# A two-layer diffusion backbone on one core: the last three steps of an attention head moved into the turn between two heads

## The chip, the cores and the metric

One core of a Trainium2 chip (trn2) runs the whole program. Its engines run side by side, and in the trace each runs its instructions in the order in which the program issued them: PE (TensorE, matrix products; PEld is its loading of weights), DVE (VectorE), ACT (ScalarE), POOL (GpSimd) and SP (which issues DMA transfers). The metric is device microseconds (us) of one execution, the median of several.

## The reference

Two layers over 512 latent tokens and 256 context tokens, width 1024, all in 32-bit floats. What matters here is the attention with two softmaxes and a difference, for 8 heads:

```python
z_lat = h_lat @ w_in[l];  kv_ctx = z_ctx[..., B_K:C_IN]       # in the last layer only k and v of the context
q, k = rope(rmsnorm(q)), rope(rmsnorm(k))                      # k of the context: rmsnorm alone
s = einsum('bqahd,bkahd->bahqk', q, k) * B_QK_DIM ** -0.5      # a: two score maps a head
p = softmax(s);  a = p[:, 0] - lam * p[:, 1]
attn = einsum('bhqk,bkhe->bqhe', a, v)                         # 768 keys for latent queries
```

In layer 0 the 256 context queries attend to the 256 context keys as well; in layer 1 there are no context queries. Around it stand a gated branch, a short convolution branch, an output projection and a feed-forward part.

## The kernel before, in words

Every product is done in three passes of split operands: a number is a rounded part ("hi") and the rest ("lo"), and hi*hi, lo*hi and hi*lo are added up. So a product of 128 rows by 8 blocks is 24 matmuls, and each operand needs a copy on ACT (the hi part) and a subtraction on DVE (the lo part). Weights stream in by DMA; the class `Stream` casts their hi part on ACT (`whi`, line 83) and subtracts for the lo part on DVE (`wlo`, line 69; the call `tick` after each step of a weave puts a pending one into DVE's queue).

The order of the work is written out by hand. Generators issue a piece of work and yield a number, its cost; `weave` (line 37) always advances the generator whose yielded sum is the smallest share of its given total. The order in which instructions are issued is the order in which each engine runs them.

In the attention of a layer, heads follow each other. While head h does its attention (`attn`, line 891), the projections of head h+1 are issued (`project`, line 1323), woven with it. `project` is: `qk_proj` (q and k for 6 blocks of 128 tokens in layer 0; in layer 1, 4 blocks and one product for the context keys, which come out the wrong way round and are transposed by `kc_tr`, lines 673 to 678), then `v_proj` in eight pieces (four of 6 matmuls with 512 columns, four of 6 with 256; called pieces 1 to 8 below), and between those pieces, on DVE, `qk_norm` (12 or 13 tiny instructions), and three `qk_rope` (called rope 0, 1, 2). Then comes a turn (line 1340): `qk_tr` transposes the three parts of q and k on PE, ACT copies the hi part, DVE subtracts (line 729), and SP issues DMAs that build a swapped copy of q (`qw`, line 733). The turn is woven with one half of the short convolution branch (`fill`), which is plain PE work.

`attn` goes through tiles of 128 queries (4 of them in layer 1, 6 in layer 0, called tile 0, 1, ...). Step i does, in this order: `av` of the pair of tiles that ends with tile i-4 (odd tiles only; 18 matmuls in turns hi, lo, hi: lines 886, 887, 888; 6 matmuls for the context pair); `to_at` of tile i-3 (6 transposes on PE, line 874; ACT copies the hi part `ah`, line 878; DVE subtracts the lo part `al`, line 879); `scores` of tile i (8 matmuls, line 841; minimum on DVE, line 848; exponentials on ACT, line 850); `combine` of tile i-1 (DVE, lines 859 to 862). So with n tiles the steps run to n+3, and the last three have only `av` and `to_at` left. `ah` and `al` have one buffer. PE's results of all these pieces, score maps aside, share four banks of PSUM (pool `pmm`, line 1307), and a bank is free again when ACT and DVE have read it.

Of the kernel before, what the change touches and what calls it, by code (L numbers as in the profile page):

```python
# [3 lines left out]

# [1 line left out]

# [5 lines left out]
F32 = mybir.dt.float32  # L12
# [8 lines left out]
NL, NC, T, D = 512, 256, 768, 1024  # L21
# [12 lines left out]
N_VS = 2  # L34


def weave(*gens, tick=lambda: None):
    act = [[g, 0.0, float(tot)] for g, tot in gens]
    while act:
        act.sort(key=lambda e: e[1] / e[2])  # L40
        e = act[0]
        try:
            e[1] += next(e[0])
        except StopIteration:
            act.remove(e)
        tick()
# [83 lines left out]
class Net:  # L130
# [34 lines left out]
    def tick(self, n):  # L165
        for _ in islice(self.bg, n):
            pass
# [713 lines left out]
    def av(self, st, kt0, nkt, yb, t0):  # L881
# [6 lines left out]
            nc.tensor.matmul(po[:, :256], lhsT=vl, rhs=st["ah"][:, i, :], start=False, stop=(i == nkt - 1))  # L888
        nc.scalar.copy(yb[:, t0:t0 + 256], po[:, :256])

    def attn(self, l, h, pool, st):
        yb = self.slots.tile([128, T], F32, tag=f"A{h}", name="yb")
        self.yb[h] = yb
        seq = [(0, 0, T), (128, 0, T), (256, 0, T), (384, 0, T)]
        if l == 0:
            seq += [(512, 512, NC), (640, 512, NC)]

        n = len(seq)
        sc, am = {}, {}
        cost = self.attn_costs(l)  # L900
        for i in range(n + 4):
            left = cost[i]
            if i >= 4 and (i - 4) % 2:
                tt, kk, nn = seq[i - 4]
                self.av(st, kk // 128, nn // 128, yb, tt - 128)
                yield 1000
                left -= 1000
            if 0 <= i - 3 < n:
                self.to_at(st, am.pop(i - 3), seq[i - 3][2], (i - 3) % 2, pool)
                yield 700  # L910
                left -= 700
            if i < n:
                sc[i] = self.scores(pool, st, *seq[i])
            if 0 <= i - 1 < n:
                am[i - 1] = self.combine(*sc.pop(i - 1))
            if i == 0:
                for c in self.v_tr(l, h, pool, st):
                    yield c
                    left -= c
            yield left  # L920

    @staticmethod
    def attn_costs(l):
        return [3200] + [2200] * 3 + [1800] * 4 if l else [3200] + [2000] * 9

    def subln(self, l, pool):
        nc = self.nc
# [308 lines left out]
    def run(self):  # L1236
# [13 lines left out]
        with tc.tile_pool(name="const", bufs=1) as const, tc.tile_pool(name="w", bufs=1) as wp, \  # L1250
# [17 lines left out]
            for l in range(2):  # L1268
                t = const.tile([128, PC_N], F32, name=f"pc{l}")
# [24 lines left out]
            for l in range(2):  # L1294
                segs = S_LAT if l else S_FULL
                ap = None
# [10 lines left out]
                with tc.tile_pool(name="attn", bufs=1) as ap, tc.tile_pool(name="pmm", bufs=4, space=PSUM) as self.mm, \  # L1307
                        tc.tile_pool(name="ps", bufs=2, space=PSUM) as self.sp:
                    self.ws.late = True
                    st = [dict(h=h) for h in range(8)]  # L1310
                    tick = self.ws.low

                    def fill(count):
                        while count:
                            g = next(cgen, None)
                            if g is None:
                                return
                            yield from g
                            count -= 1

                    chalf = 7800 if l == 0 else 5200

                    def project(h):
                        yield from self.qk_proj(l, h, ap, st[h])
                        vp = self.v_proj(l, h, ap, st[h])
                        yield next(vp)
                        if l:
                            st[h]["kc"]()
                            yield next(vp)
                        if h == 0:  # L1330
                            self.attn_lam(l, ap, tabs[0])
                        self.qk_norm(l, h, ap, st[h])
                        yield next(vp)
                        yield next(vp)
                        for c in range(3):
                            st[h]["rope", c] = self.qk_rope(l, c, ap, st[h])
                            yield next(vp)
                        yield from vp

                    def turn(h):  # L1340
                        weave((self.qk_tr(l, h, ap, st[h]), 6800), (fill(1), chalf), tick=tick)

                    p0 = project(0)
                    for i in range(8):
                        if gb:
                            next(gb)
                        next(p0)
                        tick()
                        if i == 5:
                            self.attn_setup(l, ap, *tabs)  # L1350
                    weave((p0, 15000), (fill(1), chalf), tick=tick)
                    turn(0)
                    for h in range(8):
                        a = self.attn(l, h, ap, st[h]), sum(self.attn_costs(l))
                        if h < 7:
                            weave(a, (project(h + 1), 23500), tick=tick)
                            turn(h + 1)
                        else:
                            weave(a, (fill(99), (1 + N_VS) * 10.4 * (512 if l else 768)), tick=tick)
                self.ws.low()  # L1360
                self.ws.late = False
                mmp = psum_all()
# [26 lines left out]
                n = sum(s[1] for s in self.segs)  # L1389
                for k in range(8):  # L1390
                    t = xp.tile([128, T], F32, tag=f"x{k}", name="x")
# [158 lines left out]
```

## Time and profile before

| | |
|---|---|
| median of 3 runs (range) | 2700.38 us (2697.53 to 2700.61) |
| the profiled execution, its span | 2700.74 us, 2699.0 us |
| PE busy | 2618.6 us (97%) |
| DVE busy | 1661.3 us (62%) |
| ACT busy | 1011.8 us (37%) |
| attention, layer 0: turns of heads 0 to 7 begin | 111 us to 508 us, some 57 us apart |
| attention, layer 1: turns of heads 0 to 7 begin | 1652 us to 1976 us, some 46 us apart |

How to read it: busy times are unions of the instructions of an engine. The end of a matmul in the profile is modelled, and matmuls overlap in the pipeline, so distances between starts are used where exact stretches matter: in an undisturbed stream a matmul with 512 columns starts 0.23 us after the one before, one with 256 columns 0.12 us. Idle time is put down to what ended it.

### The profile page before, as it was taken

What the parts mean: (1) busy time and instruction counts of PE and PEld (TensorE: products, weight loads), DVE (VectorE), ACT (ScalarE), POOL (GpSimd) and SP (SyncE); (2) the same over time, 40 slices, a digit from 0 to 9 for tenths busy, and PEclk for the clock granted to TensorE, in tenths of its full rate; (3) what the DMA queues carried; (4) which work ended last, traced back from release to release, by engine and by line L of the source; (5) the groups of instructions that cost most, each with busy time, mean ns of one, the idle gap of its engine ahead of it and who ended that gap; (6) DMA issues with size and microseconds to landing.
All of it is one profiled execution on the core that took longest, in us unless ns stands there. A gap on an engine that the chain in (4) does not pass through costs nothing.

```text
span 2699.0 us, 37119 instructions
## 1 busy us (share of the span) xinstructions
PE 2618.6 (97%) x14952; PEld 2267.2 (84%) x14952; DVE 1661.3 (62%) x2895; ACT 1011.8 (37%) x1711; POOL 220.6 (8%) x202
## 2 busy tenths in 40 slices
PE   7999999999999999999999999999999999999999
PEld 3988888888888888888888878898877888888887
DVE  5676777756555547544544567878777555654544
ACT  3454445452112224322322335455554232342332
POOL 0000000001111110100100100000001122020101
PEclk9999999999999999999999999999999999999999
DMA  5211122114333331222222232211225545223233
GB/s 222 81 44 51 50 59 70 50 54 141 118 112 115 110 141 55 77 80 77 77 81 78 77 103 75 64 58 54 69 67 169 175 164 177 74 94 102 94 102 110
DMA packets 80941, 254.36 MB, mean 94 GB/s; under 512 B 10480, under 2 KB 20992, under 8 KB 80384
## 3 DMA queue, kind: packets, MB, share of 16 engines
q1 hardware_dynamic: 65792, 196.64, 22.6%
q0 software_dynamic: 14544, 55.07, 6.3%
q8 instruction: 118, 1.93, 0.3%
q14 instruction: 55, 0.45, 0.1%
q10 hardware_dynamic: 432, 0.27, 0.0%
HBM read 234.63 MB, written 6.82 MB: 89 GB/s over the span
## 4 chain that ended last, share of the span: by engine, by line
PE 84%; DVE 8%; ACT 4%; DMA 2%; issue 1%; SPq 0%; POOL 0%; ACTq 0%; DVEq 0%; POOLq 0%
PE mm L183 22%; PE mm L186 22%; PE mm L184 22%; PE S L841 3%; PE mm L647 2%; PE mm L648 2%; PE mm L649 2%; DVE wlo L69 2%; DVE al L879 1%; ACT pa L850 1%; PE mmT L887 1%; ACT whi L83 1%; PE mmT L888 1%; PE mmT L886 1%; DMA wraw<-w 1%
## 5 line engine op out<-in xcount | busy, mean ns | idle before, releaser
L183 PE MATMUL mm<-hh,whi 128*128 128x512 f32 (+1 forms) x2392 | 859.7, 359 | 13.4 <-ACT hh L376 11.4
L184 PE MATMUL mm<-hl,whi 128*128 128x512 f32 (+1 forms) x2392 | 822.2, 354 | 4.4 <-DVE hl L379 4.1
L186 PE MATMUL mm<-hh,wlo 128*128 128x512 f32 (+1 forms) x2392 | 754.8, 354 | 1.6 <-DVE wlo L69 1.6
L183 PEld LDWEIGHTS mm<-hh,whi 128*128 128x128 f32 x2392 | 454.3, 190 | 106.4 <-ACT hh L376 16.3
L184 PEld LDWEIGHTS mm<-hl,whi 128*128 128x128 f32 x2392 | 454.5, 190 | 69.4 <-DVE hl L379 9.8
L69 DVE TENSOR_TENSOR wlo<-wraw,whi 128x1024 fp32r<-128x1024 f32 x320 | 399.0, 1247 | 153.1 <-ACT whi L83 151.3
L186 PEld LDWEIGHTS mm<-hh,wlo 128*128 128x128 f32 x2392 | 416.0, 191 | 42.4 <-DVE wlo L69 3.7
L83 ACT CAST whi<-wraw 128x1024 fp32r<-128x1024 f32 x320 | 334.7, 1047 | 296.3 <-PE mm L184 249.8
L1003 DVE SCALAR_TENSOR_TENSOR cv<-mm,pc,cv 128x511 f32<-128x511 f32 (+1 forms) x132 | 86.8, 657 | 181.8 <-ACT cv L1002 180.8
L850 ACT ACTIVATE pa<-S,mn 128x768 f32<-128x768 f32 (+1 forms) x160 | 129.2, 812 | 163.2 <-DVE mn L848 139.7
L183 PE MATMUL mm<-ah,whi 128*128 128x512 f32 (+1 forms) x528 | 188.0, 356 | 0.0
L647 PE MATMUL mm<-whi,hh 128*128 128x256 f32 x640 | 184.2, 288 | 1.3 <-DVE cp L778 0.8
L649 PE MATMUL mm<-whi,hl 128*128 128x256 f32 x640 | 181.0, 283 | 0.0
L648 PE MATMUL mm<-wlo,hh 128*128 128x256 f32 x640 | 181.0, 283 | 0.0
L184 PE MATMUL mm<-al,whi 128*128 128x512 f32 (+1 forms) x528 | 180.0, 354 | 0.0
L186 PE MATMUL mm<-ah,wlo 128*128 128x512 f32 (+1 forms) x528 | 161.7, 355 | 0.0
L1002 ACT ACTIVATE cv<-mm,pc 128x512 f32<-128x512 f32 (+1 forms) x132 | 88.6, 704 | 177.0 <-PE mm L186 177.0
L1164 DVE SCALAR_TENSOR_TENSOR x<-mm,mod,x 128x512 f32<-128x512 f32 (+1 forms) x91 | 58.2, 659 | 139.7 <-PE mm L186 139.7
L1207 POOL TENSOR_TENSOR cv<-cv 128x768 f32<-128x768 f32 (+1 forms) x44 | 91.8, 2087 | 606.6 <-DVE cv L1005 420.7
L647 PEld LDWEIGHTS mm<-whi,hh 128*128 128x128 f32 x640 | 122.2, 191 | 3.2 <-ACT cp L776 1.0
L648 PEld LDWEIGHTS mm<-wlo,hh 128*128 128x128 f32 x640 | 122.5, 191 | 0.1
L649 PEld LDWEIGHTS mm<-whi,hl 128*128 128x128 f32 x640 | 122.3, 191 | 0.0
(232 smaller groups left out, 4049.9 us busy)
## 6 DMA issues: line engine op xcount, KB each, us to landing
wraw<-w SPq DMA_DIRECT2D x320, 512.0 KB, 3.6
araw<-ada POOLq DMA_DIRECT2D x80, 512.0 KB, 4.0
qw<-qk SPq DMA_DIRECT2D x160, 64.0 KB, 2.0
araw<-ada SPq DMA_DIRECT2D x16, 512.0 KB, 7.8
x<-xT SPq DMA_DIRECT2D x8, 384.0 KB, 5.9
srow<-sscr POOLq DMA_DIRECT2D x3, 1024.0 KB, 7.4
x<-xT POOLq DMA_DIRECT2D x8, 384.0 KB, 6.3
xscr<-x SPq DMA_DIRECT2D x8, 256.0 KB, 4.0
```

The source lines that it names most:

```text
L69: self.lo_eng.tensor_tensor(lo, raw, hi.bitcast(F32), ALU.subtract)
L83: self.nc.scalar.copy(hi, raw)
L183: nc.tensor.matmul(ps[:, :m], lhsT=hh, rhs=xh[:, o:o + m], start=st, stop=False)
L184: nc.tensor.matmul(ps[:, :m], lhsT=hh, rhs=xl[:, o:o + m], start=False, stop=False)
L186: nc.tensor.matmul(ps[:, :m], lhsT=hl, rhs=xh[:, o:o + m], start=False, stop=sp)
L647: nc.tensor.matmul(ps[:, :256], lhsT=hh[:, sl], rhs=hi[:, c:c + 256], start=(k == 0), stop=False)
L648: nc.tensor.matmul(ps[:, :256], lhsT=hh[:, sl], rhs=lo[:, c:c + 256], start=False, stop=False)
L649: nc.tensor.matmul(ps[:, :256], lhsT=hl[:, sl], rhs=hi[:, c:c + 256], start=False, stop=(k == 7))
L850: nc.scalar.activation(pa[:, :nk], ss[a], AF.Exp, bias=mn[:, a:a + 1], scale=-1.0, accum_out=sm[a])
L1002: nc.scalar.activation(dst[:, o:o + m], s, AF.Identity, scale=w[1], bias=bias)
L1003: nc.vector.scalar_tensor_tensor(dst[:, o + 1:o + m], s[:, :m - 1], w[0], dst[:, o + 1:o + m], ALU.mult, ALU.add)
L1207: nc.gpsimd.tensor_tensor(cs[1][:, :n], cs[1][:, :n], cs[0][:, :n], ALU.mult)
```

## The change

`attn` now ends after step n (its last `combine`). The three steps that only hold `av` and `to_at` become a generator of their own, `attn_tail`, which the turn of the next head weaves with `qk_tr` and `fill`. For the last head of a layer, which has no next turn, `attn` and the tail follow each other as before, in one weave with what is left of `fill`. The costs that steer the weaves change: each step of `attn` counts 2000 (step 0: 3200), in both layers, so 15200 in layer 0 and 11200 in layer 1 against 23500 for the projections of the next head (before: 21200 and 17000); the tail counts 8000; `qk_tr` counts 5200 where it counted 6800. In layer 1 the transposes of the context keys are issued after piece 2 of `v_proj` where they were after piece 1, and `qk_norm` after piece 3 where it was after piece 2; the ropes stay where they were. No instruction is added or removed.

```diff
+    def attn_step(self, l, i, pool, st):
+        seq = self.attn_seq(l)
+        n = len(seq)
+        sc, am = st["sc"], st["am"]
+        if i >= 4 and i % 2:
+            tt, kk, nn = seq[i - 4]
+            self.av(st, kk // 128, nn // 128, st["yb"], tt - 128)
+            yield 1000
+        if 0 <= i - 3 < n:
+            self.to_at(st, am.pop(i - 3), seq[i - 3][2], (i - 3) % 2, pool)
+            yield 700
+        if i < n:
+            sc[i] = self.scores(pool, st, *seq[i])
+        if 0 <= i - 1 < n:
+            am[i - 1] = self.combine(*sc.pop(i - 1))
+
     def attn(self, l, h, pool, st):
...
+        for i in range(n + 1):
+            left = 2000
+            for c in self.attn_step(l, i, pool, st):
+                yield c
+                left -= c
             if i == 0:
                 for c in self.v_tr(l, h, pool, st):
-                    yield c
-                    left -= c
+                    yield 600
+                left += 0
             yield left
 
-    @staticmethod
-    def attn_costs(l):
-        return [3200] + [2200] * 3 + [1800] * 4 if l else [3200] + [2000] * 9
+    def attn_cost(self, l):
+        return 2000 * (len(self.attn_seq(l)) + 1) + 1200
+
+    def attn_tail(self, l, pool, st):
+        n = len(self.attn_seq(l))
+        for i, left in ((n + 1, 2600), (n + 2, 4000), (n + 3, 1400)):
+            for c in self.attn_step(l, i, pool, st):
+                yield c
+                left -= c
+            yield left
...
                         yield next(vp)
                         if l:
+                            yield next(vp)
                             st[h]["kc"]()
                             yield next(vp)
...
                         self.qk_norm(l, h, ap, st[h])
                         yield next(vp)
-                        yield next(vp)
+                        if not l:
+                            yield next(vp)
...
                     def turn(h):
-                        weave((self.qk_tr(l, h, ap, st[h]), 6800), (fill(1), chalf), tick=tick)
+                        g = [(self.attn_tail(l, ap, st[h - 1]), 8000)] if h else []
+                        weave(*g, (self.qk_tr(l, h, ap, st[h]), 5200), (fill(1), chalf), tick=tick)
...
-                        a = self.attn(l, h, ap, st[h]), sum(self.attn_costs(l))
+                        a, cost = self.attn(l, h, ap, st[h]), self.attn_cost(l)
                         if h < 7:
-                            weave(a, (project(h + 1), 23500), tick=tick)
+                            weave((a, cost), (project(h + 1), 23500), tick=tick)
                             turn(h + 1)
                         else:
-                            weave(a, (fill(99), (1 + N_VS) * 10.4 * (512 if l else 768)), tick=tick)
+                            a = chain(a, self.attn_tail(l, ap, st[h]))
+                            weave((a, cost + 8000), (fill(99), (1 + N_VS) * 10.4 * (512 if l else 768)), tick=tick)
```

## Rows read from the trace of the kernel before

**Rows 1.** The page, busy time of the engines (share of the span, instructions).

```profile
PE 2618.6 (97%) x14952; PEld 2267.2 (84%) x14952; DVE 1661.3 (62%) x2895; ACT 1011.8 (37%) x1711; POOL 220.6 (8%) x202
```

**Rows 2.** The waits of the seven whole head periods of layer 0 (120 to 518 us): who waited for whom, us in total, times, longest.

```profile
PE mmT L886 <- ACT ah L878: 11.2, 7, 1.6
PE mmT L887 <- DVE al L879: 11.2, 7, 1.6
```

**Rows 3.** The same of the seven head periods of layer 1 (1660 to 1982 us).

```profile
PE mmT L887 <- DVE al L879: 6.6, 7, 1.0
PE mmT L676 <- ACT kc L671: 4.2, 7, 0.6
PE S L841 <- DMA qw<-qk: 3.5, 6, 1.0
```

**Rows 4.** Timeline of PE in layer 0 near the end of head 1 (start us, duration us; in brackets idle time before it and what ended it).

```profile
208.05 0.40 PE L186 MATMUL mm<-hh,wlo 128*128 128x512 f32 x1
210.05 0.39 PE L886 MATMUL mmT<-ah,vh 128*128 128x256 f32 x1 [1.60 <-ACT ah L878]
212.03 0.58 PE L887 MATMUL mmT<-al,vh 128*128 128x256 f32 x1 [1.59 <-DVE al L879]
```

**Rows 5.** Timelines of DVE and of ACT in the same stretch.

```profile
209.56 0.69 DVE L638 TENSOR_REDUCE ss<-sq 128x8 f32<-128x512 f32 x1 [2.11 <-ACT sq L637]
210.16 1.22 DVE L69 TENSOR_TENSOR wlo<-wraw,whi 128x1024 fp32r<-128x1024 f32 x1
211.29 1.01 DVE L879 TENSOR_TENSOR al<-mmT,ah 128x512 fp32r<-128x512 f32 x2
...
206.63 0.47 ACT L850 ACTIVATE pa<-S,mn 128x256 f32<-128x256 f32 x1 [1.41 <-DVE mn L845]
207.55 1.04 ACT L83 CAST whi<-wraw 128x1024 fp32r<-128x1024 f32 x1
```

**Rows 6.** Windows of 12 us from the second `av` of a head on: busy us and instructions of PE, PEld, DVE, ACT, POOL, then the granted TensorE clock (share of full speed), DMA share and GB/s. The first and the last of the seven turns of layer 0 (three of the seven read 0.86, four 0.72), and one of layer 1.

```profile
151.00:163.00 12.00, 8.81 (x41) 7.12 (x40) 6.34 (x22) 3.57 (x8) 0.00 (x0) 0.86 0.15 44
...
491.00:503.00 12.00, 8.80 (x36) 7.37 (x35) 6.10 (x22) 3.57 (x9) 0.00 (x0) 0.72 0.14 44
1742.00:1754.00 12.00, 10.44 (x63) 8.79 (x62) 11.64 (x20) 5.66 (x11) 0.00 (x0) 1.00 0.29 87
```

**Rows 7.** Timeline of DVE in layer 1 over the end of a head: a minimum of scores, `combine`, the first of `qk_norm`, its last, rope 0, the `al` of the last tile, rope 1, rope 2.

```profile
1720.67 0.96 DVE L848 TENSOR_REDUCE mn<-S 128x1 f32<-128x768 f32 x1
...
1727.67 1.81 DVE L848 TENSOR_REDUCE mn<-S 128x1 f32<-128x768 f32 x2
...
1729.85 1.02 DVE L862 SCALAR_TENSOR_TENSOR pa<-pa,c 128x768 f32<-128x768 f32 x1
...
1735.31 0.06 DVE L687 MEMSET ss<- 128x4 f32 x1
...
1737.80 0.18 DVE L163 SCALAR_TENSOR_TENSOR rsy<-rst,rsy 128x24 f32<-128x24 f32 x1
...
1740.62 0.68 DVE L697 TENSOR_TENSOR zs<-zs,rsy 128x512 f32<-128x512 f32 x1
...
1743.35 1.02 DVE L879 TENSOR_TENSOR al<-mmT,ah 128x512 fp32r<-128x512 f32 x2
1744.28 0.68 DVE L697 TENSOR_TENSOR zs<-zs,rsy 128x512 f32<-128x512 f32 x1
...
1747.00 0.42 DVE L697 TENSOR_TENSOR zs<-zs,rsy 128x256 f32<-128x256 f32 x1
```

**Rows 8.** Timeline of PE in the same stretch: the first score matmul of a tile and what follows its eight; piece 4 of `v_proj`, the transposes of tile 2, the first matmul of piece 5, that of piece 6, the first two of the last `av`, and the first transpose of the turn.

```profile
1719.78 0.51 PE L841 MATMUL S<-qk 128*128 128x512 f32 x2
...
1721.16 0.29 PE L647 MATMUL mm<-whi,hh 128*128 128x256 f32 x1
...
1736.99 0.40 PE L183 MATMUL mm<-hh,whi 128*128 128x512 f32 x1
...
1738.38 0.82 PE L874 MATMUL mmT<-ident,pa 128*128 128x128 f32 x6
1738.95 0.37 PE L183 MATMUL mm<-hh,whi 128*128 128x256 f32 x1
...
1740.62 0.36 PE L183 MATMUL mm<-hh,whi 128*128 128x256 f32 x1
...
1742.85 0.28 PE L886 MATMUL mmT<-ah,vh 128*128 128x256 f32 x1
1744.08 0.39 PE L887 MATMUL mmT<-al,vh 128*128 128x256 f32 x1 [0.95 <-DVE al L879]
...
1746.22 0.60 PE L721 MATMUL mmT<-ident,ry 128*128 128x128 f32 x4
```

**Rows 9.** Timeline of DVE in a turn of layer 0: rope 2, the lo part of a weight, the six subtractions of `qk_tr`.

```profile
226.49 0.69 DVE L697 TENSOR_TENSOR zs<-zs,rsy 128x512 f32<-128x512 f32 x1
...
227.82 1.22 DVE L69 TENSOR_TENSOR wlo<-wraw,whi 128x1024 fp32r<-128x1024 f32 x1
229.07 4.29 DVE L729 TENSOR_TENSOR qk<-mmT,qk 64x512 fp32r<-64x512 f32 x6
```

**Rows 10.** Timeline of PE in the last head of layer 0 and of layer 1: an `av` that waits.

```profile
547.87 0.38 PE L886 MATMUL mmT<-ah,vh 128*128 128x256 f32 x1 [0.44 <-ACT ah L878]
...
2002.85 0.38 PE L886 MATMUL mmT<-ah,vh 128*128 128x256 f32 x1 [0.41 <-ACT ah L878]
```

More of the change, by code (lines that the diff above doesn't have):

```diff
@@ L2 @@
 from contextlib import ExitStack
-from itertools import islice
+from itertools import chain, islice
 import numpy as np
@@ L889, in av, with attn_seq @@
         nc.scalar.copy(yb[:, t0:t0 + 256], po[:, :256])
-    def attn(self, l, h, pool, st):
[L892 to L915, printed above, removed]
+    def attn_seq(self, l):
+        return [(t, 0, T) for t in range(0, NL, 128)] + ([(t, 512, NC) for t in (512, 640)] if l == 0 else [])
@@ L916, in attn @@
+    def attn(self, l, h, pool, st):
+        st["yb"] = self.yb[h] = self.slots.tile([128, T], F32, tag=f"A{h}", name="yb")
+        st["sc"], st["am"] = {}, {}
+        n = len(self.attn_seq(l))
[4 more added lines that the diff above has]
+                left -= c
             if i == 0:
                 for c in self.v_tr(l, h, pool, st):
-                    yield c
-                    left -= c
+                    yield 600
+                left += 0
@@ L920, in attn @@
             yield left
-    @staticmethod
-    def attn_costs(l):
-        return [3200] + [2200] * 3 + [1800] * 4 if l else [3200] + [2000] * 9
+    def attn_cost(self, l):
+        return 2000 * (len(self.attn_seq(l)) + 1) + 1200
+    def attn_tail(self, l, pool, st):
+        n = len(self.attn_seq(l))
+        for i, left in ((n + 1, 2600), (n + 2, 4000), (n + 3, 1400)):
[3 more added lines that the diff above has]
+            yield left
```

## The prediction

> **What bounds the kernel now.** I read the busy times first: PE is busy for 97% of the span, DVE for 62% [rows 1]. So the time is that of PE's stream, and a change of order can only touch what PE waits for. Next the waits of the two attention stretches. In layer 0 PE waits 14 times, twice a head, for the operands of an `av`: 11.2 us for `ah`, 11.2 us for `al` [rows 2]. In layer 1 three waits come back each head: `al` before the last `av` (6.6 us), the copy of the context keys (4.2 us), the DMAs of the swapped q before the first scores (3.5 us) [rows 3]. These idle times are short by the modelled ends of matmuls, so I take starts where rows show them: in layer 0, 208.05 to 210.05 to 212.03 is 2.00 + 1.98 us where an undisturbed stream would take 0.23 + 0.12, so 3.63 us a turn [rows 4]; in layer 1, 1742.85 to 1744.08 is 1.23 - 0.12 = 1.11 us [rows 8], where rows 3 show 6.6 / 7 = 0.94. I add 0.17 us to each of the 20 waits of rows 3: 14.3 + 3.4 = some 18 us, 2.6 us a turn. Last, the granted clock: in the 12 us after these `av` it is 0.86 or 0.72 in layer 0, and 1.00 in layer 1 [rows 6]. With the two levels 1.2 and 2.4 GHz that is 3.4 or 6.7 us at the half, which costs half of it: 1.7 or 3.4 us; over seven turns 3 x 1.7 + 4 x 3.4 = 18.5 us, 2.65 a turn. **At stake** are 7 x (3.63 + 2.65) = 44 us in layer 0 and 18 us in layer 1.
>
> Why PE waits there is the point to keep. Layer 0: `al` of tile 3 starts at 211.29, behind a reduction and a weight's lo part that DVE began at 209.56 [rows 5]. Layer 1: `al` of tile 3 starts at 1743.35, when rope 0, begun at 1740.62, is done [rows 7]. PE waits for the queue of DVE, not for a dependency that is long in itself. So I ask for each `av` of the new order: what stands in DVE's queue before its `al`, and how much PE work is issued in the meantime?
>
> **Layer 1, where the order gets worse.** I count the yields. Scores of tile 3 come when attention stands at 7900/11200 = 0.705, just after piece 3 of `v_proj` (16994/23500 = 0.723). Step 4, with `to_at` of tile 1, has to wait for 9200/11200 = 0.821, which is after piece 6 (0.836); then pieces 7 and 8, and the turn opens with `av` of tiles 0 and 1, because all shares start at zero and the tail is named first. So DVE's queue from there holds: minimum of tile 3, combine of tile 2, `qk_norm`, rope 0, rope 1, and only then `al` of tile 1. Before, `al` of tile 1 stood ahead of `qk_norm` and both ropes.
> - DVE, from the first score matmul of tile 3: the minimum begins 1720.67 - 1719.78 = 0.89 us later; from its begin to the end of combine 1729.85 + 1.02 - 1727.67 = 3.20; `qk_norm` 1737.80 + 0.18 - 1735.31 = 2.67; rope 0 1743.35 - 1740.62 = 2.73; rope 1 1747.00 - 1744.28 = 2.72; from the start of `al` to the matmul that reads it 1744.08 - 1743.35 = 0.73 [rows 7, 8]. Sum: 12.9 us.
> - PE, from the same matmul: scores 1721.16 - 1719.78 = 1.38; piece 4 1738.38 - 1736.99 = 1.39; six transposes 0.57; pieces 5 to 8 at (1742.85 - 1740.62) / 3 = 0.74, so 2.97; the first `av` matmul 0.12 [rows 8]. Sum: 6.4 us.
>
> PE then stands for **6.5 us** in line 887, and all that could have covered it (the transposes of `qk_tr`, `fill`) is queued behind it on PE. Bounds: 5.5 us if DVE gets ahead by a us, 7.5 if a pending weight's lo part (1.22 us [rows 5]) slips in before `al`.
>
> On top comes the clock. Layer 0's waits of 3.63 us in two parts were followed by the half clock in seven turns of seven, layer 1's single 1.1 us never [rows 4, 6, 8]; 6.5 us in one piece is on layer 0's side. I take 2.5 us a turn, between 1.7 and 3.4 (0 if it does not fall). The Trainium skill speaks against the change at this point: its page "TensorE: Matmul & The Clock Gate", section "HAM oscillation — how this bites in real kernels", says that bursts of matmuls with long enough stalls between them each begin at the half rate, so that the price is paid once per repetition and not once in all. By it seven turns pay; with no such price the sum below would be 17 us less. Rows 6 agree for layer 0.
>
> Gained in layer 1: the 2.6 us. The context keys have one more piece (1.39 us) ahead of their transposes, against a wait of 0.6 idle; the last `av` now stands behind `fill`; the first scores have DVE's subtractions and SP's eight DMAs of q done earlier, since PE comes later. Small new waits in the turn for PSUM banks that DVE has not yet read, up to 1 us, lie inside the time at the half clock. So a turn of layer 1 costs 6.5 + 2.5 - 2.6 = +6.4 us, seven of them **+45 us** (bounds 3.9 x 7 = 27 and 7.9 x 7 = 55). Head 0's context keys also come one piece later, before the first turn: between 0 and 1.39 us, I take +1.
>
> **Layer 0, where it helps a little.** By the yields, `to_at` of tile 3 comes after piece 4, scores of tile 5 just before it, then pieces 5 to 8, and `av` of tiles 2 and 3 opens the turn. From the end of the sixth q/k block:
> - PE: scores of tile 4 0.5, pieces 1 and 2 2.8, `av` 2.1, piece 3 1.4, transposes 0.6, piece 4 1.4, scores of tile 5 0.5, transposes 0.6, four pieces 3.0: 12.9 us to `av`.
> - DVE: reduction of the block 2.0 us after it (207.55 to 209.56 on ACT and DVE), with a weight's lo part 1.73 [rows 5]; minimum of tile 4 0.6 (two thirds of layer 1's 0.96, an estimate from half the elements and more), combine 1.4, `qk_norm` 2.6, `al` of tile 2 0.9, rope 0 2.7, minimum 0.6 [rows 7]: 12.5. The two exponentials of tile 5 hold ACT 0.92 us [rows 5], then `ah` of tile 3, some 0.6; `al` starts at 14.2, and PE goes on at 15.0.
>
> PE waits 2.1 us instead of 3.63. Then comes something new. `to_at` of tile 5 is the fourth user of a bank while `fill` holds one, so it needs the bank of the first `qk_tr`, which DVE frees behind `al` of tile 3 (0.9), rope 1 (2.7), combine (0.9), rope 2 (1.33), a lo part (1.25) and two subtractions (1.43) [rows 7, 9]: 14.2 + 8.5 = 22.7. PE gets there at 15.0 + 2.14 for `av` [rows 8] + 0.4 + 1.4 + 0.25 + 1.4 + 0.4 = 21.0. That wait, 1.7 us, and the half clock, 2.5, cover each other, as a slower PE arrives later: 2.1 + 2.5 = 4.6 against 6.3. So -1.6 us a turn, **-11 us** (bounds: -20 when one of the two falls away, 0 when DVE is 1.5 us later).
>
> **Last heads.** `fill` runs out at two thirds in both versions; the first `av` that waits now [rows 10] stands behind one or two pieces of `fill`. I take -1 us each, -2 us.
>
> **Sum**, against the profiled execution of 2700.74 us (span 2699.0, 1.7 around it, 0.4 above the median): 2700.7 + 45 + 1 - 11 - 2 = 2733.7, so 2734 us.
>
> **Rivals.**
> - *All waits hidden* (the other side, faster). The place is DVE's queue between the scores of tile 3 and the turn. It decides whether `al` of tile 1 is ready in 6.4 us. If so, 18 + 44 + 2 us go: 2637 us; with layer 0 as above and layer 1 clean, 2700.7 - 18 - 11 - 2 = 2670. For it: DVE is idle for 38% of the span, and of the `av` of a head only one waited in layer 1 [rows 3]. Against it: the 12.9 us are a plain sum of rows of one queue. Chance 0.11, for both forms.
> - *The wait without the clock.* Layer 1: 6.5 + 1.0 for banks - 2.6 = 4.9, so +34; layer 0: 2.1 + 1.7 - 6.3 = -2.5, so -17: 2700.7 + 34 - 17 - 1 = 2717 us. For it: the granted clock stays at 1.00 after the waits of layer 1 [rows 6]. Against: layer 0's seven of seven. Chance 0.12.
> - *Layer 0 gains nothing*, since banks and ropes take back what the `av` gains, and each turn of layer 1 pays 3.4 us for the clock: 2700.7 + 51 = 2752 us. Chance 0.09.
> - *The move does not do what it says* for the context keys: ACT's copy stands behind two exponentials there too, and the wait stays, 7 x 0.8 us: +5 us, inside the range. No chance of its own.
>
> **How the numbers follow.** Forecast 2734 us, chance 0.68, its own range 2722 to 2746. The range 2704 to 2753 takes in the second and third rival and the bounds of layer 1 (27 - 20 - 2 = +5 us and 55 - 2 = +53 us); outside it I leave the fast rival (0.11) and some hundredths above. About 0.2% (5.4 us) is what a measurement of this kernel can tell from no change: faster 0.11, same 0.05, slower 0.84.
>
> **What would show it.** Right: in layer 1 seven waits of PE in line 887 for `al`, each 5 to 7 us, at the opening of the turn, `al` of tile 1 behind rope 1 on DVE, granted clock under 1 after it; no wait at line 676; none for `qw`. In layer 0 the waits at lines 886 and 887 sum to 2 us a turn instead of 3.6, and a new one before the transposes of line 874 on DVE's line 729. Wrong: if line 887 waits less than 2 us in layer 1, then DVE had done the ropes by then, and the forecast falls to the first rival; if clock stays at 1.00 there, the second holds.

## The result and the profile after

The changed kernel takes 2733.23 us (median of 4 runs, 2732.44 to 2734.57), the kernel before 2700.49 us beside it: ratio 1.0123, 95% interval 1.0105 to 1.0141. That is 33 us slower, where 2734 us was forecast. The profiled execution has a span of 2730.7 us.

The page: over the whole program PE's busy time hardly moved. That sum hides two changes that nearly cancel, as the rows of the two layers show below: in layer 0 PE's busy time fell, in layer 1 it rose.

```profile
PE 2615.6 (96%) x14952; PEld 2269.3 (83%) x14952; DVE 1667.0 (61%) x2895; ACT 1013.0 (37%) x1711; POOL 220.9 (8%) x202
```

PE's waits in layer 1, heads 0 to 6 (1643 to 2010 us; us in total, times, longest), to be read beside [rows 3]:

```profile
PE mmT L887 <- DVE al L879: 44.5, 7, 6.4
PE mmT L721 <- DVE qk L729: 8.4, 12, 0.8
PE S L841 <- DMA qw<-qk: 0.3, 1, 0.3
```

The wait for the context keys is gone (4.2 us before), that for the DMAs of q nearly so, and line 887 has gone from 6.6 to 44.5 us, with seven waits in both (before, of the last `av` of a head; now of the first, which opens the turn). The 8.4 us before the transposes of q and k (line 721) are new.

PE in one turn of layer 1 (start us, duration, idle time before it):

```profile
1720.30 0.51 PE L841 MATMUL S<-qk 128*128 128x512 f32 x2
...
1724.52 0.82 PE L874 MATMUL mmT<-ident,pa 128*128 128x128 f32 x6
...
1726.61 0.28 PE L886 MATMUL mmT<-ah,vh 128*128 128x256 f32 x1
1733.24 0.58 PE L887 MATMUL mmT<-al,vh 128*128 128x256 f32 x1 [6.35 <-DVE al L879]
...
1737.04 1.05 PE L721 MATMUL mmT<-ident,ry 128*128 128x128 f32 x4
...
1740.90 0.63 PE L721 MATMUL mmT<-ident,ry 128*128 128x128 f32 x4 [0.30 <-DVE qk L729]
```

and DVE in the same stretch: minimum, `combine`, `qk_norm`, rope 0, rope 1, `al` of tile 1, and later the subtractions of the first transposes:

```profile
1721.19 1.82 DVE L848 TENSOR_REDUCE mn<-S 128x1 f32<-128x768 f32 x2 [0.48 <-PE S L841]
...
1723.38 1.02 DVE L862 SCALAR_TENSOR_TENSOR pa<-pa,c 128x768 f32<-128x768 f32 x1
1724.34 0.06 DVE L687 MEMSET ss<- 128x4 f32 x1
...
1726.83 0.18 DVE L163 SCALAR_TENSOR_TENSOR rsy<-rst,rsy 128x24 f32<-128x24 f32 x1
1727.05 0.69 DVE L697 TENSOR_TENSOR zs<-zs,rsy 128x512 f32<-128x512 f32 x1
...
1729.78 0.69 DVE L697 TENSOR_TENSOR zs<-zs,rsy 128x512 f32<-128x512 f32 x1
...
1732.50 1.01 DVE L879 TENSOR_TENSOR al<-mmT,ah 128x512 fp32r<-128x512 f32 x2
...
1739.34 1.41 DVE L729 TENSOR_TENSOR qk<-mmT,qk 64x512 fp32r<-64x512 f32 x2 [2.52 <-ACT qk L726]
```

Read the two together. From the first score matmul at 1720.30 the chain runs to 1733.24, 12.94 us: DVE takes up the first scores 0.89 us later and from there works through its queue without a wait, piece for piece the durations that were added up (0.89, 3.21, 2.67, 2.73, 2.72, 0.74). PE has 6.31 us of work to 1726.61, issues one matmul and stands 6.5 us. The same instructions of `al` for tile 1 took no time from anyone before, because they stood ahead of `qk_norm`.

PE's waits in layer 0, heads 0 to 6 (120 to 500 us), beside [rows 2]:

```profile
PE mmT L874 <- DVE qk L729: 12.1, 7, 1.7
PE mmT L886 <- ACT ah L878: 6.9, 7, 1.0
PE mmT L887 <- DVE al L879: 2.4, 7, 0.3
```

They sum to 21.4 us; before it was 22.4. By starts it is no less either. PE in the second of the seven turns of layer 0:

```profile
212.10 0.28 PE L186 MATMUL mm<-hh,wlo 128*128 128x256 f32 x1
213.37 0.39 PE L886 MATMUL mmT<-ah,vh 128*128 128x256 f32 x1 [0.99 <-ACT ah L878]
214.09 0.39 PE L887 MATMUL mmT<-al,vh 128*128 128x256 f32 x1 [0.34 <-DVE al L879]
...
219.65 0.60 PE L721 MATMUL mmT<-ident,ry 128*128 128x128 f32 x4
221.99 0.41 PE L874 MATMUL mmT<-ident,pa 128*128 128x128 f32 x2 [1.74 <-DVE qk L729]
```

The three distances, less 0.12, 0.12 and 0.36 us (what the four transposes take elsewhere in this turn), are waits of 1.15 + 0.60 + 1.98 = 3.73 us; before the change they were 3.63. So layer 0 hardly waits less. It is still faster, and the granted clock says why. Windows of 12 us over the turns (last columns but two: granted clock): the first and the last turn of layer 0, then two of layer 1, beside [rows 6].

```profile
157.00:169.00 12.00, 8.95 (x56) 7.54 (x55) 10.88 (x22) 6.96 (x16) 0.00 (x0) 1.00 0.16 44
484.00:496.00 12.00, 8.95 (x55) 7.51 (x55) 10.92 (x21) 6.61 (x16) 0.00 (x0) 1.00 0.19 62
...
1733.00:1745.00 12.00, 10.71 (x53) 9.52 (x54) 8.28 (x16) 4.64 (x10) 0.00 (x0) 0.75 0.28 93
1786.00:1798.00 12.00, 9.81 (x54) 8.69 (x55) 8.84 (x17) 4.78 (x10) 0.00 (x0) 0.83 0.27 71
```

In layer 0 the clock stays at 1.00, in all seven turns, where it read 0.86 and 0.72; in layer 1 it falls where it stayed.

How much each layer gave can be read from whole head periods: seven of them lie between the first score matmul (line 841) of head 0 and that of head 7. Windows from the one to the other, layer 0 and layer 1, in the kernel before:

```profile
120.91:518.24 397.33, 374.18 (x2578) 347.64 (x2577) 293.21 (x566) 195.08 (x430) 0.00 (x0) 0.95 0.19 54
1660.68:1982.47 321.79, 306.76 (x2116) 279.09 (x2114) 255.92 (x495) 168.77 (x348) 0.00 (x0) 1.00 0.20 61
```

and in the changed kernel:

```profile
120.31:500.68 380.37, 358.97 (x2578) 334.24 (x2577) 296.95 (x568) 195.20 (x430) 0.00 (x0) 1.00 0.20 58
1642.15:2015.35 373.20, 319.25 (x2116) 293.97 (x2115) 262.38 (x498) 168.97 (x347) 0.00 (x0) 0.93 0.18 53
```

Layer 0 gained 397.33 - 380.37 = 17.0 us. PE runs the same 2578 matmuls in 15.2 us less busy time, and its idle time fell by only 1.8 us (23.2 to 21.4). Layer 1 lost 373.20 - 321.79 = 51.4 us: 12.5 us more busy time for the same 2116 matmuls at a lower clock, and 38.9 us more idle time.

### The profile page after: what moved, and what is told of

Its sections match the earlier page's. It is cut to its first block, busy times and chain, and to the rows that moved or that the text cites. A ratio compares the mean times of both kernels' runs of the same rounds, so it can differ in the third digit from the quotient of the medians.

```text
span 2730.7 us, 37064 instructions
## 1 busy us (share of the span) xinstructions
PE 2615.6 (96%) x14952; PEld 2269.3 (83%) x14952; DVE 1667.0 (61%) x2895; ACT 1013.0 (37%) x1711; POOL 220.9 (8%) x202
## 3 DMA queue, kind: packets, MB, share of 16 engines
q1 hardware_dynamic: 65792, 196.64, 22.4%
## 4 chain that ended last, share of the span: by engine, by line
PE 83%; DVE 11%; ACT 2%; DMA 2%; issue 2%; POOL 0%; DVEq 0%; ACTq 0%; SPq 0%; POOLq 0%
PE mm L183 22%; PE mm L186 22%; PE mm L184 22%; PE S L841 3%; PE mm L647 3%; PE mm L649 3%; PE mm L648 3%; DVE wlo L69 1%; DMA wraw<-w 1%; DVE qk L729 1%; DVE zs L697 1%; PE mmT L887 1%; DVE al L879 1%; PE mmT L874 1%; PE mmT L888 1%
## 5 line engine op out<-in xcount | busy, mean ns | idle before, releaser
L848 DVE TENSOR_REDUCE mn<-S 128x1 f32<-128x768 f32 x128 | 116.5, 951 | 45.6 <-PE S L841 45.5
```

The lines of the kernel that those rows point to most:

```text
L848: nc.vector.tensor_reduce(mn[:, a:a + 1], ss[a], AX.X, ALU.min)
```

## The experiments

Two theories were put against each other. The queue theory is that of the prediction: what costs is what stands in DVE's queue ahead of an operand, against the PE work issued meanwhile. Its rival: the turn itself is the wrong place, as three generators share it, whatever DVE's queue holds. Times of different runs are compared by their ratios to the kernel before on the same chip; one per mille is 2.7 us.

**1. Layer 0 alone changed.** Layer 1 has the steps, costs and keys of before:

```diff
+        if l:
+            cost = [3200] + [2200] * 3 + [1800] * 4
+            for i in range(n + 4):
+                left = cost[i]
...
-                        g = [(self.attn_tail(l, ap, st[h - 1]), 8000)] if h else []
+                        g = [(self.attn_tail(l, ap, st[h - 1]), 8000)] if h and not l else []
```

> The change in layer 0 alone; layer 1 keeps the order of before, context keys included. Queue theory (in layer 1 the lo part of tile 1 stands behind the ropes in DVE's queue, in layer 0 the queue is shorter than PE's work): layer 0 keeps its gain of about 20 us and layer 1 loses nothing, 2681 us (2674 to 2688). Rival, that the time is lost in the turn itself because three generators share it, in either layer: 2700 us or more.

Measured: 2682.26 us, ratio 0.9942 (0.9928 to 0.9955), 16 us faster than before. So in layer 0 the turn is no wrong place for the tail. By difference, 1.0123 - 0.9942 = 0.0181, or 49 us, is what the new order of layer 1 costs (51.4 by the head periods of the two traces above). The traces bear out that the layers can be taken apart: the seven head periods of layer 0 take 380.35 us here and 380.37 us in the changed kernel, and those of layer 1 take 321.20 us here and 321.79 us before.

**2. Layer 0 and the context keys.** The same, and in layer 1 the keys transposed a piece later, as in the change.

```diff
                         if l:
+                            yield next(vp)
                             st[h]["kc"]()
...
-                        yield next(vp)
+                        if not l:
+                            yield next(vp)
                         for c in range(3):
```

> As the run with layer 0 alone, with the context keys of layer 1 transposed one piece later as well. Queue theory: the seven waits of PE for the copied keys (0.77 us each by starts) go and qk_norm has slack on DVE, so about 5 us less than with layer 0 alone, 2676 us. Rival, that the later qk_norm pushes the ropes and is part of the loss in layer 1: the same as with layer 0 alone or up to 7 us more.

Measured: 2677.91 us, ratio 0.9924 (0.9911 to 0.9938): 4.9 us less than run 1 by the ratios, though their intervals overlap. The rows settle it: the seven head periods of layer 1 take 316.43 us, 4.8 us less than in run 1. PE's waits of layer 1 without the later keys (run 1) hold

```profile
PE mmT L676 <- ACT kc L671: 4.3, 7, 0.6
```

and with them (run 2) the line is not there, while the wait in the `av` is as before:

```profile
PE mmT L887 <- DVE al L879: 6.6, 7, 1.0
PE S L841 <- DMA qw<-qk: 4.7, 7, 0.9
```

The later `qk_norm` costs nothing here, so it is no part of the loss.

**3. The lo part ahead of the ropes, the tail still in the turn.** In layer 1 the attention counts more in its weave, so its steps come earlier:

```diff
-                            weave((a, cost), (project(h + 1), 23500), tick=tick)
+                            weave((a, 14000 if l else cost), (project(h + 1), 23500), tick=tick)
```

> The changed kernel, but in layer 1 the attention counts 14000 instead of 11200 in its weave, so the transposes of tile 1 come after piece 2 of the v projection and its lo part stands ahead of qk_norm and the ropes on DVE; the tail stays in the turn. Queue theory: the 6.5 us wait at the opening of the turn goes to nearly 0; DVE still has qk_norm, three ropes and a weight's lo part to do before the subtractions of the turn, so waits of about 4 us come at the transposes of q and k instead: 2695 to 2710 us. Rival, that the tail's place in the turn is what costs: 2725 us or more.

Measured: 2704.95 us, ratio 1.0021 (1.0012 to 1.003). 28 us of the loss are gone with one number in a weave. PE's waits in layer 1:

```profile
PE mmT L721 <- DVE qk L729: 26.0, 9, 3.5
PE mmT L721 <- DVE ry L706: 6.9, 7, 1.0
```

Line 887 has no wait left. DVE's queue, in which the ropes now come after `al`, holds up the transposes of q and k, 32.9 / 7 = 4.7 us a turn (some 4 expected): rope 0 for the first of them, and the bank that DVE has not read yet for the second.

**4. The branch work first.** The generators of the turn in layer 1 in the opposite order, so PE has something to do before the `av`:

```diff
-                        weave(*g, (self.qk_tr(l, h, ap, st[h]), 5200), (fill(1), chalf), tick=tick)
+                        gens = [*g, (self.qk_tr(l, h, ap, st[h]), 5200), (fill(1), chalf)]
+                        weave(*(gens[::-1] if l else gens), tick=tick)
```

> The changed kernel, but in the turn of layer 1 the branch work goes first, then the first transposes of q and k, then the AV product. Queue theory: DVE finishes at the same time, PE has 1.4 us of branch work and 0.4 us of transposes in front, so the waits before and in the AV product sum to about 4.7 us instead of 6.5 and the time falls by 10 to 13 us, to 2720 to 2723 us. Rival, that the loss is the clock and not the wait: the clock still falls in each turn and the time stays within 4 us of 2733.

Measured: 2719.16 us, ratio 1.0075 (1.0061 to 1.0088), 13 us less than the change. PE's waits in layer 1:

```profile
PE mmT L886 <- DVE al L879: 18.3, 7, 2.6
PE mmT L721 <- DVE ry L706: 12.9, 7, 1.9
PE mmT L721 <- DVE qk L729: 7.6, 12, 0.8
```

The first two sum to 31.2 / 7 = 4.5 us a turn (4.7 expected), 44.5 / 7 = 6.4 before the swap. (Line 886 does not read `al`. It writes to a bank, so what it waits for must be the bank that `al` is the last to read.) The window 1728 to 1740 us shows the clock at 0.86, so part of the 13 us is a shorter stretch at the half clock, not waiting alone.

```profile
1728.00:1740.00 12.00, 7.10 (x38) 5.88 (x38) 11.50 (x22) 2.80 (x6) 0.00 (x0) 0.86 0.24 64
```

**5. The suspected queue made longer.** Two instructions of rope 1 are done two times more, four instructions in all, with the same values; nothing is added on PE. (Four lines are new above line 887, which is 891 here.)

```diff
             nc.vector.tensor_tensor(t2[:, :, :, 32:64], zn[:, :, :, 0:32], sg[:, :, :, 32:64], ALU.mult)
+            if l and c == 1 and h:
+                for _ in range(2):
+                    nc.vector.tensor_tensor(t2[:, :, :, 0:32], zn[:, :, :, 32:64], sg[:, :, :, 0:32], ALU.mult)
+                    nc.vector.tensor_tensor(t2[:, :, :, 32:64], zn[:, :, :, 0:32], sg[:, :, :, 32:64], ALU.mult)
```

> The changed kernel with four of DVE's instructions in rope 1 of layer 1 done again (the same values once more, heads 1 to 7): 4 x 0.34 = 1.4 us more on DVE ahead of the lo part of tile 1, none on PE. Queue theory: PE's wait at the opening of the turn grows from 6.5 to 7.9 us, and the whole of it reaches the time: 7 x 1.4 = 10 us more, 2743 us. Rival, that the tail's place in the turn costs whatever DVE's queue holds: no change, 2733 us.

Measured: 2742.31 us, ratio 1.0159 (1.0145 to 1.0172): 9.7 us more than the change (10.5 us more in the seven head periods), and PE's wait

```profile
PE mmT L891 <- DVE al L883: 53.9, 7, 7.7
```

grew by 9.4 us in total. Work on an engine that is busy 61% of the span reaches the time nearly one for one, at this place.

**6. PE kept busy while it waits.** 48 matmuls into an unread half of the bank, before the first `av` of the tail in layer 1:

```diff
+        for _ in range(extra):
+            nc.tensor.matmul(po[:, 256:512], lhsT=st["vh"][:, 0, :], rhs=st["ah"][:, 0, :], start=True, stop=True)
         for i in range(nkt):
...
+            self.av(..., 48 if l and i == 5 and st["h"] < 7 else 0)
```

> The changed kernel with 48 matmuls of 256 columns, whose results nobody reads, before the first AV product of the tail in layer 1 (heads 0 to 6): 48 x 0.12 = 5.8 us of PE work inside the 6.5 us of waiting, so that PE works while it waits for DVE. If the clock's fall is a price of its own, it stays at full rate and each turn is 2.5 us faster, 2713 to 2718 us. If DVE's queue sets the end of the turn too (the banks that the next transposes wait for), a PE at full rate only waits longer there: 2728 to 2736 us, with longer waits before the transposes of q and k.

Measured: 2720.22 us, ratio 1.0074 (1.0061 to 1.0086). Neither number: the time falls by 13 us, or 1.9 us a turn, between the two. Windows over one turn show the clock kept up, and PE's waits of layer 1 what remains:

```profile
1728.00:1740.00 12.00, 11.31 (x88) 10.57 (x86) 11.14 (x25) 2.92 (x6) 0.00 (x0) 1.00 0.12 35
1734.00:1746.00 12.00, 9.83 (x63) 8.32 (x62) 10.04 (x19) 5.79 (x12) 0.00 (x0) 1.00 0.34 101
```

```profile
PE mmT L721 <- DVE qk L729: 10.8, 14, 0.8
PE mmT L889 <- DVE al L879: 4.3, 7, 0.6
```

So the half clock has a price of its own, 1.9 us a turn, and only a little of it was covered: the bank waits grew from 8.4 to 10.8 us. The 12.5 us that the change added to PE's busy time in layer 1 agree with it.

**7. One transpose later in layer 0.** Run 2 with other costs in the tail, so that `to_at` of tile 5 comes after the third piece of branch work:

```diff
-        for i, left in ((n + 1, 2600), (n + 2, 4000), (n + 3, 1400)):
+        for i, left in ((n + 1, 3600), (n + 2, 3000), (n + 3, 1400)):
```

> Layer 0 changed and layer 1 as before but for the keys (2678 us), and in layer 0 the transposes of tile 5 one piece of branch work later in the turn, by counting 3600 and 3000 instead of 2600 and 4000 for the first two tail steps. Bank theory: the wait of 1.9 us for DVE's subtractions of the first q and k part shrinks by one piece, 1.4 us, in seven turns, 5 to 10 us faster: 2668 to 2673 us. Rival, that DVE is simply late in the whole turn: the wait moves to the next transposes and the time stays at 2678 us.

Measured: 2670.62 us, ratio 0.989 (0.9877 to 0.9904), 9 us less than run 2 by the ratios. The bank wait fell from 12.1 to 2.2 us and did not come back elsewhere in layer 0 (the transposes of line 874 do not read `qk`, so what they wait for DVE's line 729 to free is a bank); the other two are as in the changed kernel:

```profile
PE mmT L886 <- ACT ah L878: 6.9, 7, 1.0
PE mmT L887 <- DVE al L879: 2.4, 7, 0.3
PE mmT L874 <- DVE qk L729: 2.2, 7, 0.3
```

**8. Layer 0's attention earlier.** Run 7, and in layer 0 the attention of heads 0 to 6 counts 18200 in its weave:

```diff
-                            weave((a, cost), (project(h + 1), 23500), tick=tick)
+                            weave((a, cost if l else 18200), (project(h + 1), 23500), tick=tick)
```

> As the run with the later transpose (2671 us), and in layer 0 the attention of heads 0 to 6 counts 18200 instead of 15200 in its weave, so the transposes of tile 3 come before piece 3 of the v projection and its lo part stands ahead of the ropes on DVE. By the queue theory PE's waits at the opening of the turn in layer 0 (1.75 us by starts: 1.15 for the hi part, 0.6 for the lo part) go, and half or so comes back at the transposes that wait for DVE's subtractions, since DVE's own work up to them is shorter by two pieces at most: 2658 to 2666 us. If DVE's queue alone sets the end of the turn, all of it comes back there: 2671 us.

Measured: 2662.5 us, ratio 0.9866 (0.9849 to 0.9882). The only wait of PE left in layer 0's turns is

```profile
PE mmT L874 <- DVE qk L729: 7.5, 7, 1.1
```

The 9.3 us at the `av` are gone, 5.3 us came back at the bank. This version is 1.3% faster than the kernel before and 2.5% faster than the change (0.9866 / 1.0123 = 0.975).

## Why the prediction came out

The total, 33 us by forecast and 33 us measured, came out closer than its terms, and that closeness is luck. By the seven head periods of each layer, layer 1 lost 51.4 us where 45 were forecast and layer 0 gained 17.0 where 11 were: two misses of 6 us, in opposite directions. The last heads (from the first scores of head 7 to the last matmul of its `av`) gained 1.1 and 0.6 us, 1 and 1 forecast. The four sum to +32.7 us. The mechanism of the largest term, the wait in layer 1, was right.

- **The wait in layer 1** was right: 6.5 us by a sum over DVE's queue and PE's work; the trace shows 1733.24 - 1726.61 - 0.12 = 6.5, and each link of the chain within 0.02 us. That this queue is the cause is shown, not only argued: with `al` ahead of the ropes the wait goes (run 3), with more work in front of PE it shrinks (run 4), with 1.4 us more on DVE it grows by as much (run 5).
- **The clock in layer 1** fell, as forecast, but was priced at 2.5 us a turn; run 6 gives 1.9, and the busy time of PE 12.5 / 7 = 1.8.
- **The bank waits in layer 1** were put at nothing beyond the clock, on the ground that they lie inside the time at the half clock. That step failed. They are 8.4 / 7 = 1.2 us a turn of idle time and even 10.8 / 7 = 1.5 at the full clock. The reason is in the rows of the turn: the bank's chain starts with PE itself. The first transposes go at 1737.04, DVE waits 2.52 us for ACT's copies of them, ends its subtractions at 1739.34 + 1.41 = 1740.75, and the next transposes follow at 1740.90. A later PE takes that chain along with it: from the first transposes to the next it is 3.86 us here at the half clock, and 3.42 us in run 6 at the full clock.
- **The bounds of layer 1**, 3.9 and 7.9 us a turn, do not follow from the terms beside them: the longest wait and the dearest clock give 7.5 + 3.4 - 2.6 = 8.3, the shortest wait without the clock 5.5 - 2.6 = 2.9. The measured 51.4 / 7 = 7.3 lies inside either.
- **The keys and the gain in layer 1**: the wait at line 676 went as forecast, worth 4.9 us (run 2), and `qw` nearly went. Head 0's +1 us cannot be told from the traces: the stretch from the end of layer 0's attention to the first scores of layer 1 takes between 1106 and 1110 us in the traces of the ten kernels, with no order between those with the later keys and those without.
- **Layer 0's waits** came near where they were put: by starts 1.15 + 0.60 = 1.75 us at the `av`, with 2.1 forecast, and 1.98 at the bank, with 1.7. Run 7 shows that the second hangs on the work in front of it: one more piece takes it away. Most of what is left at the `av`, 6.9 of 9.3 us, is for `ah`, as the forecast had it: `ah` stands in ACT's queue behind two exponentials, and these had waited 2.81 us for a minimum that DVE takes after rope 0. The sentence that PE waits for the queue of DVE leaves ACT's queue out: before the change half of the 22.4 us in layer 0 was for `ah` [rows 2].
- **Layer 0's clock** was the failed term: 2.5 us a turn were expected for another fall, and it did not fall at all. That is why layer 0's seven periods gained 17.0 us and not 11: 15.2 us of it is busy time of PE, and the waits are as long as before. The price of the clock before the change was put a little too high, because the 12 us windows count half-clock time in which PE only waited: of the 37.5 us at 0.50 in those seven turns PE was busy for 34.0, half of which is 17.0 us and not 18.5.

The rival with all waits hidden is out by the wait of 44.5 us; the rival without the clock is out in layer 1 by the windows at 0.75 and 0.83, though its term for layer 0, -17, is what was measured there. The one that gave layer 0 nothing is out by run 1.

What stays open: for layer 1 a run shows the price of the clock (run 6), for layer 0 only the account of busy and idle time does. No run holds layer 0's new order and lowers the clock, and why the clock stayed up there is not shown.

## What to carry to other kernels

For each matmul that reads a split or copied operand, add up two columns from rows of the trace before you move it: what stands in the producing engine's queue ahead of that operand, and how much work the consuming engine has been given meanwhile; the difference is the wait, to 0.1 us in layer 1 and 0.4 us in layer 0, however idle the producing engine is on average. Moving work to a place with cover is no gain if its operand's producer moves behind a longer job on the way: here one number in a weave's cost table took back 28 of the 33 us lost (run 3). With layer 1 left in its old order but for the keys, and two more such settings in layer 0 (runs 7 and 8), the same idea gained 36 us. A wait for a PSUM bank whose chain begins on the waiting engine was not hidden here by slowing that engine.

## What the runs showed of the hardware that was not expected

The granted clock does not follow the sum of waits in a turn. In layer 0 before, two waits of 1.77 and 1.86 us with a single matmul between them were followed by the half clock in seven turns of seven [rows 4, 6]. After the change 1.75 us (0.99 and 0.34 us idle by the profile), then some 6 us of work, then 1.98 us (1.74 idle) left it at 1.00 in all seven. In run 3 waits of the same lengths, 0.98 and 3.49 us, at the same places of the order, gave different clocks in different turns. Two turns, from their first transposes on:

```profile
1725.00:1737.00 12.00, 7.72 (x44) 6.32 (x45) 10.21 (x19) 5.84 (x11) 0.00 (x0) 1.00 0.37 107
1773.60:1785.60 12.00, 8.46 (x41) 7.11 (x42) 9.77 (x18) 5.28 (x11) 0.00 (x0) 0.86 0.31 84
```

The Trainium skill, "TensorE: Matmul & The Clock Gate", section "HAM oscillation — how this bites in real kernels", has each burst after a long stall begin at the half rate. Layer 1 of the changed kernel agrees (0.75 and 0.83 after 6.5 us); layer 0 before falls as well although no single wait there reached 2 us. And 5.8 us a turn of matmuls that compute nothing of use made this kernel 13 us faster than the change without them.
